# Moving the split weights by 64 bytes within SBUF

## The chip, the core and the metric

The kernel runs on one core of a Trainium2 chip. The metric is the device time of one execution, in microseconds (us); 1 ns is a thousandth of it. The profile of one execution shows what each engine did: TensorE (PE; its weight loads are PEld), VectorE (DVE), ScalarE (ACT), GpSimd (POOL) and SyncE (SP, which only issues DMAs).

## What is computed

One layer of a hybrid decoder for 576 tokens (512 of a prompt and 8 samples of 8), model width 1024, all in float32:

```
u   = rms(x) * g_pre_mix
z, xbc, dt, q, k, v, ig, fg, og = split(u @ w_in)       # one input projection
y_ssd = Mamba2-SSD heads(xbc, dt) gated by z;  h_ml = mLSTM heads(q, k, v, ig, fg) gated by og
x   = x + rms(concat(y_ssd, h_ml) @ w_out) * g_post_mix  # output projection
mk, mv = rms(mem) * g_mem @ w_mem_k, ... @ w_mem_v       # memory keys and values of the prompt
x   = x + rms(attention(rms(x) @ w_xq, mk, mv) @ w_xo) * g_post_x
x   = x + rms((silu(u @ w_gate) * (u @ w_up)) @ w_down) * g_post_ffn
```

The samples also read and update recurrent states and cached keys and values. The outputs are the new x, the memory keys and values and all new states.

## The kernel before

Nearly all of the work is matrix products in which both operands are split: a float32 value is the sum of a high part, rounded to the type float32r, and a low part, the difference. A product of two split operands takes three matmuls per tile of 128 x 128 weights, which accumulate in PSUM: high weights with high activations, high weights with low activations, low weights with high activations. In `gemm` (lines 194 to 205) these are lines 201, 202 and 204; each one is a matmul with a weight load of its own:

```
(wh, wl), ah, al = tiles[k], xh(k, t0, n), xl(k, t0, n)
mm(ps, wh, ah, start=i == 0, stop=False)
mm(ps, wh, al, start=False, stop=False)
```

In `mm(out, a, b)` the operand `a` is the stationary one (loaded into the array, 128 columns of 4 bytes) and `b` the moving one (streamed through it, `n` columns). In most products the weights are stationary and the activations move. In the memory values (lines 794 to 796) and in the mLSTM values v (line 814) the weights are the moving operand.

The 576 tokens are taken in two parts, of 256 and 320 columns, or, in the attention's output projection and the gated MLP, of 288 and 288. The input projection, the two output projections' halves, the query projection and the memory keys run unit by unit: a unit is 8 weight tiles of 128 x 128 (a 512 KB load), and gives 24 matmuls for each part of the tokens. The gated MLP forms products by sums and differences of its operands in blocks (class `Seven`, with `mul` at lines 1848 to 1850); its gate and up products begin in the plain form of lines 201 to 204.

The weights come by DMA into a tile `raw` (line 174), ScalarE writes the high part `whi` (line 179) and VectorE, or for the input projection partly a DMA that accumulates, the low part `wlo` (line 186). `raw`, `whi` and `wlo` lie in the pool "weights", each tile 4096 bytes per partition, in 2, 3 and 3 buffers. Another pool holds three more `whi` and `wlo` in the later stages, and `wacc`, `w3`, `wdh` and `wdl` are split weights in other places again.

The pools are laid out in SBUF one behind the other, in the order in which they are opened: "const" (from 16512), "weights" (from 18336), and "big" (from 51104), which has the activations' slots. The pool "const" holds constants and the small tiles of the reciprocal square roots: in `newton` and `root_sums` the tiles `v`, `y` and `a` in two buffers each, of up to 20 bytes, 32 bytes apart.

The start of an operand modulo 256, in bytes per partition. A weight tile of 128 columns is 512 bytes on from the one before it, and a token tile's row of 576 or 640 columns is 2304 or 2560 bytes, so the start modulo 256 does not depend on k. The second half of 288 columns starts 1152 bytes on, so there the moving operand's start is 128 more, modulo 256.

| tile | role | start modulo 256, before | after |
|---|---|---|---|
| `whi`, `wlo` of the pool "weights" | split weights | 160 | 96 |
| `whi`, `wlo` of the later pool, `wacc`, `w3`, `wdh`, `wdl` | split weights | 160 | 160 |
| `wmh` / `wml` | a memory key's weights, split | 224 / 160 | same |
| `uh`, `ul` | input projection, activations | 160 | same |
| `mixs_h` / `mixs_l` | first output projection (SSD half) | 224 / 160 | same |
| `mixm_h`, `mixm_l` | second output projection (mLSTM half) | 160 | same |
| `u2h`, `u2l`, `memhl` | query projection, memory | 160 | same |
| `qh` / `ql` | attention's output projection | 224 / 160 | same |
| `u3h`, `u3l`, `b1`, `b5` | gate and up products | 160 | same |
| `hh` / `hl` | down products | 224 / 160 | same |

The order of the instructions on each engine comes from a scheduler that works from dependencies and a cost model, and from an order written out by hand for the last stages.

Of the kernel before, what the change touches and what calls it, by code (L numbers as in the profile page):

```python
# [11 lines left out]
F32 = mybir.dt.float32  # L12
# [7 lines left out]
P = 128  # L20
# [95 lines left out]
def build(nc, tc, ctx, I, O):  # L116
# [2 lines left out]

    cp = ctx.enter_context(tc.tile_pool(name="const", bufs=1))  # L120
    wp = ctx.enter_context(tc.tile_pool(name="weights", bufs=1))
    big = ctx.enter_context(tc.tile_pool(name="big", bufs=1))
    pg = ctx.enter_context(tc.tile_pool(name="pg", bufs=3, space=PSUM))
    pa = ctx.enter_context(tc.tile_pool(name="pa", bufs=3, space=PSUM))
# [29 lines left out]
    def C32(k):  # L154
        a, b = _c32[k]
        return c32[:, a:b] if b <= NLONG else c32e[:, a - NLONG:b - NLONG]
# [64 lines left out]
    def rstd_cols(ssq, chunks, name, d=1024.0, alloc=None):  # L221

        nch = len(chunks)
        ps = (alloc or BP)("ps_ss")
        for j in range(nch):
            for i, t_ in enumerate(ssq):
                ssq_mm.append(mm(ps[:, j:j + 1], t_[:, chunks[j][0]:chunks[j][0] + P], ones, start=i == 0,
                                 stop=i == len(ssq) - 1, skip_group_check=True))
        return newton(ps[:, :nch], [P, nch], name, d)

    def newton(src, shape, name, d):
        v = cp.tile(shape, F32, name=name + "_v", tag="nt_v", bufs=2)
        y = cp.tile(shape, F32, name=name + "_y", tag="nt_y", bufs=2)
        a = cp.tile(shape, F32, name=name + "_a", tag="nt_a", bufs=2)
        r = cp.tile(shape, F32, name=name + "_r")
        w = shape[1]
        V.tensor_scalar(v, src, 1.0 / d, EPS, op0=ALU.mult, op1=ALU.add)
        pows.append(G.tensor_tensor(y, v, C32("nhalf")[:shape[0], :w], op=ALU.pow))
        V.tensor_tensor(a, y, y, op=ALU.mult)
        V.scalar_tensor_tensor(a, a, -0.5, v, op0=ALU.mult, op1=ALU.mult)  # L240
        rops.append(V.scalar_tensor_tensor(r, a, 1.5, y, op0=ALU.add, op1=ALU.mult))
        return r
# [339 lines left out]
    y = xs  # L582
# [126 lines left out]
    for g in range(2):  # L709
# [13 lines left out]
        for h in range(8):  # L723
            k, j = h % 2, (8 * g + h) // 2
# [163 lines left out]
    for h in range(4):  # L888
        q, k = qk[:, h, :], qk[:, 4 + h, :]
# [689 lines left out]
    def root_sums(name, ssq, i, alloc):  # L1579
        ps = alloc("ps_ss")  # L1580
        for c, (t0, _) in enumerate(ECHUNKS[i]):
            mm(ps[:, c:c + 1], ssq[:, t0:t0 + P], ones, start=True, stop=True, skip_group_check=True)
        v, y, a = [cp.tile([P, 3], F32, name=name + k, tag="nt" + k, bufs=2) for k in ("_v", "_y", "_a")]
        V.tensor_scalar(v, ps[:, :3], 1.0 / 1024.0, EPS, op0=ALU.mult, op1=ALU.add)
        G.tensor_tensor(y, v, C32("nhalf")[:, :3], op=ALU.pow)
        R[name] = v, y, a
# [19 lines left out]
    def norm(name, ssq, i, out, alloc, p, d):  # L1606

        at_(p, root_sums, name, ssq, i, alloc)
        at_(p + 0.4, root_step, name)
        at_(d, root_rows, name, i, alloc)  # L1610
        at_(d + 0.2, root_copy, name, i, out)
# [744 lines left out]
```

## Time and profile before

| | |
|---|---|
| three executions | 1095.28, 1095.61 and 1095.99 us; median 1095.61 |
| span of the profiled execution | 1095.0 us, from its first instruction to its last; no other time of that execution is listed |
| busy | PE 1084.1 us, PEld 1027.5, DVE 754.0, ACT 611.7, POOL 225.8 |
| matmuls | 8124, each with a weight load |
| DMA | 182.29 MB, mean 166 GB/s |

A row of instructions in the profile gives line, engine, operation, the tile written `<-` the tiles read (moving operand first), the shape and the count, then busy time in us and the mean duration of one in ns, then the idle time before them and what ended it. A row of the timeline gives the start in us from the span's start, the duration in us, and the instruction. The duration of a matmul covers its way through the array, so it overlaps with the next one's; the distance from one start to the next, the pitch, is what it takes of the time.

### The profile page before, as it was taken

Reading aid. Unit: us, or ns where it says so; the run is one execution under the profiler, and the core shown is the slowest. Engines: PE = TensorE matmul, PEld = TensorE weight load, DVE = VectorE, ACT = ScalarE, POOL = GpSimd, SP = SyncE. Lnnn points to the kernel's source line nnn. Section 1 sums busy time; section 2 is a strip of 40 time slices with the busy share of each in tenths; the row PEclk is TensorE's granted clock in tenths of the full one; section 3 lists DMA queues with packets and bytes.
Section 4 is the critical chain, followed back from the end, with each engine's and each line's share of the span. In section 5 each row is a group of like instructions: output and inputs, shape, how many; then the busy total and the mean of one; then the engine's idle time right before and its main releaser. Section 6 shows DMA issues by size and latency. Waiting matters only on the chain.

```text
span 1095.0 us, 20715 instructions
## 1 busy us (share of the span) xinstructions
PE 1084.1 (99%) x8124; PEld 1027.5 (94%) x8124; DVE 754.0 (69%) x1507; ACT 611.7 (56%) x1098; POOL 225.8 (21%) x305
## 2 busy tenths in 40 slices
PE   9999999999999999999999999999999999999997
PEld 8999887778999999999988879999999999999997
DVE  6896785658877775558744546676566877787555
ACT  7767632455654555656545445645566566656653
POOL 1332643313213112000144301100011121111000
PEclk9999999999999999999999999999999999999999
DMA  6785635435655349653467775644386687588532
GB/s 204 170 154 127 170 111 174 163 84 177 189 149 146 106 132 312 205 189 102 150 215 271 264 248 163 217 161 109 104 195 142 150 196 173 116 188 186 128 130 88
DMA packets 58967, 182.29 MB, mean 166 GB/s; under 512 B 6605, under 2 KB 11853, under 8 KB 58357
## 3 DMA queue, kind: packets, MB, share of 16 engines
q1 hardware_dynamic: 42740, 138.06, 39.0%
q0 software_dynamic: 15552, 41.95, 19.8%
q8 instruction: 64, 1.05, 0.4%
q10 hardware_dynamic: 576, 0.95, 0.3%
q14 instruction: 35, 0.28, 0.1%
HBM read 160.28 MB, written 20.65 MB: 165 GB/s over the span
## 4 chain that ended last, share of the span: by engine, by line
PE 88%; DVE 5%; ACT 4%; DMA 2%; issue 1%; SPq 0%; POOL 0%; DVEq 0%; ACTq 0%
PE ps_v L814 5%; PE ps_in L202 4%; PE ps_in L201 4%; PE ps_in L204 4%; PE ps_o L202 3%; PE ps_o L204 3%; PE ps_o L201 3%; PE ps_g L1848 3%; PE ps_g L1849 3%; PE ps_g L1850 3%; PE ps_u L1848 3%; PE ps_u L1850 3%; PE ps_u L1849 3%; PE ps_dn L1848 2%; PE ps_dn L1849 2%; PE ps_dn L202 2%
## 5 line engine op out<-in xcount | busy, mean ns | idle before, releaser
L201 PE MATMUL ps_in<-uh,whi 128*128 128x320 f32 (+1 forms) x544 | 164.0, 302 | 0.4 <-DVE cb L450 0.4
L204 PE MATMUL ps_in<-uh,wlo 128*128 128x320 f32 (+1 forms) x544 | 163.2, 300 | 0.0
L202 PE MATMUL ps_in<-ul,whi 128*128 128x320 f32 (+1 forms) x544 | 162.7, 299 | 0.0
L179 ACT CAST whi<-raw 128x1024 fp32r<-128x1024 f32 (+1 forms) x104 | 105.2, 1013 | 96.2 <-PE ps_in L202 26.1
L186 DVE TENSOR_TENSOR wlo<-raw,whi 128x512 fp32r<-128x512 f32 (+1 forms) x96 | 96.6, 1009 | 66.5 <-ACT whi L179 65.8
L201 PEld LDWEIGHTS ps_in<-uh,whi 128*128 128x128 f32 x544 | 103.1, 190 | 3.4 <-issue 1.7
L204 PEld LDWEIGHTS ps_in<-uh,wlo 128*128 128x128 f32 x544 | 103.0, 190 | 1.2 <-issue 0.4
L202 PEld LDWEIGHTS ps_in<-ul,whi 128*128 128x128 f32 x544 | 103.1, 190 | 0.6
L184 POOL DMA_DIRECT2D wlo<-win x32 | 27.9, 871 | 80.1 <-ACT wlo L183 72.0
L1848 PE MATMUL ps_g<-b,whi 128*128 128x288 f32 x144 | 42.5, 295 | 0.0
L1849 PE MATMUL ps_g<-b,whi 128*128 128x288 f32 x144 | 42.4, 295 | 0.0
L1848 PE MATMUL ps_u<-b,whi 128*128 128x288 f32 x144 | 42.4, 295 | 0.0
L1849 PE MATMUL ps_u<-b,whi 128*128 128x288 f32 x144 | 42.4, 295 | 0.0
L1821 ACT CAST whi<-rawx 128x1024 fp32r<-128x1024 f32 (+1 forms) x26 | 25.7, 987 | 27.8 <-PE ps_dn L1849 13.8
L191 DVE TENSOR_TENSOR wlo<-sw,whi 128x1024 fp32r<-128x1024 f32 (+1 forms) x26 | 29.6, 1140 | 14.9 <-ACT whi L190 14.7
L201 PE MATMUL ps_xo<-qh,whi 128*128 128x288 f32 x128 | 38.5, 302 | 0.2 <-ACT whi L179 0.2
L202 PE MATMUL ps_o<-mixs_l,whi 128*128 128x320 f32 (+1 forms) x128 | 38.2, 299 | 0.0
L204 PE MATMUL ps_o<-mixm_h,wlo 128*128 128x256 f32 (+1 forms) x128 | 38.2, 298 | 0.0
L202 PE MATMUL ps_o<-mixm_l,whi 128*128 128x256 f32 (+1 forms) x128 | 37.9, 296 | 0.0
L201 PE MATMUL ps_xq<-u2h,whi 128*128 128x320 f32 (+1 forms) x128 | 37.9, 300 | 0.0
L201 PE MATMUL ps_o<-mixm_h,whi 128*128 128x256 f32 (+1 forms) x128 | 37.9, 296 | 0.0
L204 PE MATMUL ps_xq<-u2h,wlo 128*128 128x320 f32 (+1 forms) x128 | 37.9, 296 | 0.0
(765 smaller groups left out, 3838.9 us busy)
## 6 DMA issues: line engine op xcount, KB each, us to landing
raw<-win SPq DMA_DIRECT2D x35, 512.0 KB, 3.9
raw<-wout SPq DMA_DIRECT2D x17, 512.0 KB, 3.6
raw<-wxq SPq DMA_DIRECT2D x13, 512.0 KB, 3.6
raw<-wgate SPq DMA_DIRECT2D x13, 512.0 KB, 3.5
raw<-wup SPq DMA_DIRECT2D x13, 512.0 KB, 5.3
wlo<-win POOLq DMA_DIRECT2D x24, 256.0 KB, 5.1
kva<-kc SPq DMA_DIRECT2D x12, 512.0 KB, 5.7
kva<-vc SPq DMA_DIRECT2D x12, 512.0 KB, 6.0
```

Source lines behind the costliest of these rows:

```text
L179: casts.append(A.copy(hi[:, :n], raw[:, :n]))
L184: G.dma_start(lo[:, a:b], src[:, a:b], accum_op=ALU.add)
L186: e.tensor_tensor(lo[:, a:b], raw[:, a:b], hi[:, a:b].bitcast(F32), op=ALU.subtract)
L191: (eng or V).tensor_tensor(lo, src, hi.bitcast(F32), op=ALU.subtract)
L201: mm(ps, wh, ah, start=i == 0, stop=False)
L202: mm(ps, wh, al, start=False, stop=False)
L204: m = mm(ps, tiles[order[c]][1], xh(order[c], t0, n), start=False, stop=c == len(tiles) - 1)
L814: mm(ps, a, b, skip_group_check=True, **kw)
L1821: A.copy(s.h3[:, s.all], s.r2[:, s.all])
L1848: mm(ps, wh, b[0][k], start=start and k == 0, stop=False, skip_group_check=True)
L1849: mm(ps, wh, b[1][k], start=False, stop=False, skip_group_check=True)
L1850: m = mm(ps, wl, b[0][k], start=False, stop=k == nk - 1, skip_group_check=True)
```

## The change

A pool "newton" is opened behind "weights", and the tiles `v` of `newton` and of `root_sums`, in two buffers of 32 bytes, move there from "const". "const" becomes 64 bytes shorter, so that the few small tiles behind `v` in it and the whole pool "weights" lie 64 bytes lower: `whi`, `wlo` and `raw` start at 96 modulo 256 in place of 160. The new pool fills the 64 bytes behind "weights", and every pool after it stays where it was. The instructions and their order on each engine are the same.

```diff
     cp = ctx.enter_context(tc.tile_pool(name="const", bufs=1))
     wp = ctx.enter_context(tc.tile_pool(name="weights", bufs=1))
+    nv = ctx.enter_context(tc.tile_pool(name="newton", bufs=1))
     big = ctx.enter_context(tc.tile_pool(name="big", bufs=1))
...
     def newton(src, shape, name, d):
-        v = cp.tile(shape, F32, name=name + "_v", tag="nt_v", bufs=2)
+        v = nv.tile(shape, F32, name=name + "_v", tag="nt_v", bufs=2)
         y = cp.tile(shape, F32, name=name + "_y", tag="nt_y", bufs=2)
...
             mm(ps[:, c:c + 1], ssq[:, t0:t0 + P], ones, start=True, stop=True, skip_group_check=True)
-        v, y, a = [cp.tile([P, 3], F32, name=name + k, tag="nt" + k, bufs=2) for k in ("_v", "_y", "_a")]
+        v, y, a = [(nv if k == "_v" else cp).tile([P, 3], F32, name=name + k, tag="nt" + k, bufs=2) for k in ("_v", "_y", "_a")]
         V.tensor_scalar(v, ps[:, :3], 1.0 / 1024.0, EPS, op0=ALU.mult, op1=ALU.add)
```

## The prediction

> **What bounds the kernel now.** I read the page's busy shares, the chain that ended last, the waits of TensorE, the sums by window, and then the timeline of TensorE product by product. From the page:
>
> ```profile
> span 1095.0 us, 20715 instructions
> ...
> PE 1084.1 (99%) x8124; PEld 1027.5 (94%) x8124; DVE 754.0 (69%) x1507; ACT 611.7 (56%) x1098; POOL 225.8 (21%) x305
> ...
> PEclk9999999999999999999999999999999999999999
> ...
> PE 88%; DVE 5%; ACT 4%; DMA 2%; issue 1%; SPq 0%; POOL 0%; DVEq 0%; ACTq 0%
> ```
>
> TensorE is busy for 99% of the span, at full clock in every slice, and makes 88% of the chain. Its waits, of which the first and the last of six rows stand here, are next to nothing:
>
> ```profile
> PE ps_warm L302 <- DVE wz L299: 1.1, 1, 1.1
> ...
> PE ps_xo L201 <- ACT whi L179: 0.2, 1, 0.2
> ```
>
> So the time is the sum of the distances from the start of one matmul to the start of the next. Only a change of that pitch can move the end by much, and this change touches nothing else: all five engines issue the same instructions in the same order; some operands lie 64 bytes lower. The profiled span of 1095.0 is 0.6 under the median of 1095.61; I take differences from the profile and set them against the median.
>
> **What a pitch is made of.** "Distance" below is the start address of the moving operand less that of the stationary operand of the next matmul (which loads meanwhile), modulo 256. In the second product of the output projection, mixm_h, mixm_l and the weights all start at 160 modulo 256: distance 0. In the first, mixs_h starts at 224, so two products of three are at distance 64 and the third, of mixs_l, at 0. Both run without a stall, each unit being 24 matmuls of 256 columns and then 24 of 320. From the timeline, the first row of each run of 24 and of what follows it:
>
> ```profile
> 411.36 0.28 PE L201 MATMUL ps_o<-mixs_h,whi 128*128 128x256 f32 x1
> ...
> 414.21 0.31 PE L201 MATMUL ps_o<-mixs_h,whi 128*128 128x320 f32 x1
> ...
> 417.73 0.28 PE L201 MATMUL ps_o<-mixs_h,whi 128*128 128x256 f32 x1
> ...
> 453.13 0.28 PE L201 MATMUL ps_o<-mixm_h,whi 128*128 128x256 f32 x1
> ...
> 456.01 0.31 PE L201 MATMUL ps_o<-mixm_h,whi 128*128 128x320 f32 x1
> ...
> 459.53 0.28 PE L201 MATMUL ps_o<-mixm_h,whi 128*128 128x256 f32 x1
> ```
>
> At distance 0, 24 matmuls of 256 columns take 456.01 - 453.13 = 2.88 us, 120.0 ns each; with two in three at 64 they take 2.85 us, 118.75 each. That is 1.25 ns a matmul over all, or 1.9 ns for each one that is at 64. At 320 columns both take 3.52 us, 146.7 each: no gain. The mean durations of the groups, between 403 and 453 us, show the same and a little more:
>
> ```profile
> L202 PE MATMUL ps_o<-mixs_l,whi 128*128 128x320 f32 x53 | 16.6, 312 | 0.0
> L201 PE MATMUL ps_o<-mixs_h,whi 128*128 128x320 f32 x53 | 16.4, 309 | 0.0
> L204 PE MATMUL ps_o<-mixs_h,wlo 128*128 128x320 f32 x53 | 16.3, 308 | 0.0
> L202 PE MATMUL ps_o<-mixs_l,whi 128*128 128x256 f32 x48 | 13.7, 285 | 0.0
> L204 PE MATMUL ps_o<-mixs_h,wlo 128*128 128x256 f32 x48 | 13.4, 280 | 0.0
> L201 PE MATMUL ps_o<-mixs_h,whi 128*128 128x256 f32 x48 | 13.4, 279 | 0.0
> L201 PE MATMUL ps_o<-mixm_h,whi 128*128 128x320 f32 x16 | 4.9, 309 | 0.0
> ...
> L201 PE MATMUL ps_o<-mixm_h,whi 128*128 128x256 f32 x8 | 2.3, 283 | 0.0
> ```
>
> A duration is longer than a pitch, since matmuls overlap, but its differences can be compared. At 256 columns the products of mixs_h are 3.5 under the 283 of distance 0 and that of mixs_l is 2 over it; at 320 they are 0.5 under and 3 over. A second case at 256 columns is the memory keys: memhl at 160, weights wmh at 224 (distance 192), wml at 160; 48 matmuls:
>
> ```profile
> 496.32 0.28 PE L201 MATMUL ps_mk<-memhl,wmh 128*128 128x256 f32 x1
> ...
> 501.98 0.28 PE L794 MATMUL ps_v<-wmh,memhl 128*128 128x256 f32 x1
> ```
>
> 5.66 us over 48 is 117.9 ns, 2.1 under 120.0. At 288 columns distance 0 is not the dear one. The first half of the gate and up products has distance 0, the second, from 724.28 on, 128, since the half's offset is 1152 bytes; the output projection of the attention has 64, 0, 64:
>
> ```profile
> 717.43 0.29 PE L204 MATMUL ps_g<-u3h,wlo 128*128 128x288 f32 x1
> ...
> 724.28 0.29 PE L201 MATMUL ps_g<-u3h,whi 128*128 128x288 f32 x1
> ...
> 749.88 0.29 PE L1848 MATMUL ps_g<-u3h,whi 128*128 128x288 f32 x1
> ...
> 655.62 0.30 PE L201 MATMUL ps_xo<-qh,whi 128*128 128x288 f32 x1
> ...
> 658.40 0.29 PE L201 MATMUL ps_xo<-qh,whi 128*128 128x288 f32 x1
> ```
>
> 52 matmuls at distance 0 take 6.85 us, 131.7 each; 192 at distance 128 take 25.60, 133.3 each; 21 of the mixture take 2.78, 132.4 each.
>
> **The sum.** Counted in the two programs, pair by pair of single-pass products:
>
> - 256 columns, 0 to 64: 1469 pairs. I take 1.9 ns off each, from the unit above: -2.8 us. The ends are no gain and 2.1 (the keys): 0 to -3.1.
> - 256 columns, 0 to 192 (the memory values, where the split weights are the moving operand): 138 pairs, also 1.9: -0.3; ends 0 and -0.3.
> - 320 columns, 0 to 64: 1321 pairs. The equal 3.52 us says 0. A gain as large as the keys' 2.1 would be -2.8; the other end is the dearest run of 320 columns at 64, 0, 64, that of the last down product, below: +3.0.
> - 288 columns: 850 pairs go from 0 to 64. The run at 64, 0, 64 is 0.7 above distance 0: +0.6; the ends are 0 and the 1.6 between 131.7 and 133.3: +1.4. 596 pairs go from 128 to 192, 253 from 192 to 0, 209 from 64 to 128. By the same step of 1.6 the first two can bring -1.0 and -0.4 and the third can cost +0.3; I take -0.2 for all three.
> - 256 and 320 columns, 64 to 128, in the mixed products: 213 and 214 pairs. No row has 128 at these widths; by the step of 1.6 either way, within 0.7 us; I take 0.
> - 512 columns, 0 to 192 (the values): 203 pairs, none of them to be compared in a stream; at most 2.1 ns either way, 0.4 us; I take 0.
>
> The remaining 1340 or so pairs keep their distance: tiles of other pools, among them another pool of split weights. The sum is -2.8 - 0.3 + 0 + 0.6 - 0.2 = -2.7 us: **1092.9**.
>
> What else the move touches costs nothing in time that I can see. The casts and subtractions that fill the split weights, and their loads, keep their sizes and order; the moved tiles are 8 to 20 bytes per partition. A faster TensorE could be held up by its supply; a unit of 48 matmuls, 6.4 us, stands against these:
>
> ```profile
> L179 ACT CAST whi<-raw 128x1024 fp32r<-128x1024 f32 (+1 forms) x104 | 105.2, 1013 | 96.2 <-PE ps_in L202 26.1
> L186 DVE TENSOR_TENSOR wlo<-raw,whi 128x512 fp32r<-128x512 f32 (+1 forms) x96 | 96.6, 1009 | 66.5 <-ACT whi L179 65.8
> ...
> raw<-win SPq DMA_DIRECT2D x35, 512.0 KB, 3.9
> ```
>
> About 1 us of cast, 1 us of subtraction and 3.9 us to landing are covered by the unit in work, and 0.03 or 0.1 us less of it leaves them covered. Without cover a unit could be no faster than its load, 3.9 us, far from here.
>
> **The rivals.** *A: the gain is larger.* Once both activations lie at one distance, the stream no longer jumps between two, and the 2 and 3 ns over at mixs_l (285 and 312) may belong to the jump. Then each 256-column pair gains the 3.5 of mixs_h and each 320-column pair 0.5: 1607 x 3.5 + 1321 x 0.5 = 5.6 + 0.7, less the 0.4 lost at 288: -5.9, so 1089.7. Against it: the equal 3.52 us at 320, and the keys, where the moving operand does not jump and gains only 2.1.
>
> *B: addresses do not count.* The two operands are read without regard to each other, and the differences between stages come from something else in them. Then nothing moves: 1095.6. The memory keys speak against it, at 117.9 with an ordinary stream, as does the step from 131.7 to 133.3 within one set of products at 724.28; for it speaks the equality at 320. The Trainium skill has this as a rule: "SBUF — State Buffer", section "Who interferes with whom", gives TensorE two independent read ports, one for the moving operand and one for weight loads, and says that TensorE never waits for anyone. The trace agrees at 320 columns (3.52 us in both) and not at 256 (2.85 against 2.88).
>
> *C: slower.* Distance 64 is dear where most bytes stream, at 288 and 320 columns. The last down product has the distances 64, 0, 64 against the tile wdh; 21 matmuls of 320 columns:
>
> ```profile
> 1061.81 0.31 PE L201 MATMUL ps_dn<-hh,wdh 128*128 128x320 f32 x1
> ...
> 1064.94 0.28 PE L201 MATMUL ps_dn<-hh,wdh 128*128 128x256 f32 x1
> ```
>
> 3.13 us is 149.0 each, 2.3 above 146.7. If the 320-column pairs become like these, +3.0 us, the 288-column ones like distance 128, 850 x 1.6 = +1.4, and a stream wholly at 64 keeps the 120.0 at 256, the sum is +4.4: 1100.0. It is decided at 320 columns: with the gain of 3.1 at 256 kept and 1.4 lost at 288, it ends slower than now from 1.3 ns a pair. For it: no large product in the trace starts its weights at 96, where they will lie. Against it: the run of 24 at 64, 0, 64 in the first output projection shows no such cost, at 3.52 us.
>
> **How the numbers follow.** My forecast has 0.36, A 0.18, B 0.18, C 0.28. Each term's ends added up reach -8.0 and about +5; the range that leaves out two in ten goes from 1086 to 1100, which takes in A and C. A measurement can tell about 0.2% from no change, 2.2 us. Faster by more than that are most of the forecast (0.30), A and a little of B (0.02): 0.50. Within it are the rest of the forecast (0.06) and of B (0.16): 0.22. Slower is C: 0.28.
>
> **What would show it.** Right: the 24 matmuls of 256 columns in the second output projection take 2.84 us or less and those of 320 columns 3.52, and the first half of the gate and up products goes up from 131.7 towards 132.4. A shows as under 2.82 and under 3.50; C as over 3.55; B as 2.88 and 3.52 with 1095.6 in all. Waits of TensorE that sum to over 10 us, or a chain with less of TensorE in it, would make the whole argument wrong, since then the pitch would not set the time.

## The result and the profile after

| | before | after |
|---|---|---|
| median of ten executions each, same chip | 1096.10 us | 1093.55 us |
| ratio, 95% interval | | 0.9978 [0.9969, 0.9987] |
| span of the profiled execution | 1095.0 us | 1090.7 us |

The changed kernel is faster by 0.22%, which is close to the least that a measurement of this kernel can tell from no change; the interval excludes no change. The prediction said 1092.9. The spans show more of a gain than the medians do. The profiled execution of after took 1092.51 us, the least of its ten; and where a run lists both, the time is 1.7 to 1.9 us over the span, so the span of 1095.0 belongs to some 1096.8 us, over the median of before. A second profile of after (below) has 1092.2.

From the page of the kernel after:

```profile
span 1090.7 us, 20715 instructions
...
PE 1081.4 (99%) x8124; PEld 1024.5 (94%) x8124; DVE 753.3 (69%) x1507; ACT 611.6 (56%) x1098; POOL 227.0 (21%) x305
...
PE 90%; DVE 4%; DMA 2%; issue 2%; ACT 2%; POOL 0%; SPq 0%; DVEq 0%; ACTq 0%; POOLq 0%
```

TensorE is busy for 99% as before and has 90% of the chain (88% before). Its waits, all of them:

```profile
PE ps_warm L303 <- DVE wz L300: 1.1, 1, 1.1
PE ps_ct L554 <- ACT r L533: 0.3, 1, 0.3
PE ps_in L205 <- DMA wlo<-win: 0.2, 1, 0.2
PE ps_xo L202 <- ACT whi L180: 0.2, 1, 0.2
```

They sum to 1.8 us. Before, they summed to 3.3; these are the four rows of before that the prediction does not show:

```profile
PE ps_ss L227 <- DVE ssqx L268: 0.8, 1, 0.8
PE ps_in L338 <- ACT whi L190: 0.5, 1, 0.5
PE ps_in L201 <- DVE cb L450: 0.4, 1, 0.4
PE ps_ct L553 <- ACT r L532: 0.3, 1, 0.3
```

In the second profile of after they sum to 4.3 us. They vary from one execution to the next by about as much as the change is worth, but all are far under the 10 us that the prediction set as the sign against it: the supply of weights kept up, and the pitch still sets the time. The timeline of TensorE in after, with the first row of each run of equal products and of what follows it (lines 202, 203 and 205 are 201, 202 and 204 of before):

```profile
409.53 0.28 PE L202 MATMUL ps_o<-mixs_h,whi 128*128 128x256 f32 x1
...
412.33 0.31 PE L202 MATMUL ps_o<-mixs_h,whi 128*128 128x320 f32 x1
...
450.95 0.28 PE L202 MATMUL ps_o<-mixm_h,whi 128*128 128x256 f32 x1
...
453.77 0.31 PE L202 MATMUL ps_o<-mixm_h,whi 128*128 128x320 f32 x1
...
457.30 0.28 PE L202 MATMUL ps_o<-mixm_h,whi 128*128 128x256 f32 x1
...
493.79 0.28 PE L202 MATMUL ps_mk<-memhl,wmh 128*128 128x256 f32 x1
...
499.45 0.28 PE L795 MATMUL ps_v<-wmh,memhl 128*128 128x256 f32 x1
...
713.88 0.29 PE L202 MATMUL ps_u<-u3h,whi 128*128 128x288 f32 x1
...
720.60 0.29 PE L202 MATMUL ps_g<-u3h,whi 128*128 128x288 f32 x1
...
746.19 0.30 PE L1849 MATMUL ps_g<-u3h,whi 128*128 128x288 f32 x1
...
1057.55 0.31 PE L202 MATMUL ps_dn<-hh,wdh 128*128 128x320 f32 x1
...
1060.67 0.28 PE L202 MATMUL ps_dn<-hh,wdh 128*128 128x256 f32 x1
```

In the second output projection (mixm) the 24 matmuls of 256 columns take 453.77 - 450.95 = 2.82 us (2.88 before), and the 24 of 320 columns 3.53 (3.52). In the first (mixs) the 256 columns take 2.80 (2.85). The memory keys, whose addresses did not change, take 5.66 us, as before. The first half of the gate and up products takes 6.72 us over 51 matmuls, 131.8 ns each (131.7), the second 25.59 over 192, 133.3 each (133.3). The last down product, unchanged too, takes 3.12 us over 21 (3.13). The gain sits at 256 columns, as forecast.

Where time was won and where it was lost is seen in the groups by form. In the input projection at 256 columns a matmul of the high parts went from 288 to 286 ns; in the mLSTM values, where the weights stream 512 columns, it went from 404 to 408. Two rows of before, then two of after (line, engine, operation, count, then busy us and mean ns of one):

```profile
L201 PE MATMUL ps_in<-uh,whi 128*128 128x256 f32 x272 | 78.2, 288 | 0.0
L814 PE MATMUL ps_v<-whi,uh 128*128 128x512 f32 x80 | 32.2, 404 | 0.0
```

```profile
L202 PE MATMUL ps_in<-uh,whi 128*128 128x256 f32 x272 | 77.7, 286 | 0.1
L815 PE MATMUL ps_v<-whi,uh 128*128 128x512 f32 x80 | 32.5, 408 | 0.0
```

Worked out over all starts in the two traces, matmul by matmul, with the pairs that stall in either trace left out:

| columns, distance before to after | pairs | pitch before, ns | after, ns | us in all | forecast, us |
|---|---|---|---|---|---|
| 256, 0 to 64 | 1431 | 120.35 | 118.16 | -3.13 | -2.8 |
| 256, 0 to 192 | 135 | 121.24 | 118.09 | -0.43 | -0.3 |
| 320, 0 to 64 | 1300 | 147.80 | 147.48 | -0.41 | 0 |
| 288, 0 to 64 | 849 | 132.36 | 132.11 | -0.21 | +0.6 |
| 288, 128 to 192, 192 to 0, 64 to 128 | 1050 | | | -0.41 | -0.2 |
| 256 and 320, 64 to 128 | 426 | | | +0.10 | 0 |
| 512, 0 to 192 | 199 | 234.51 | 237.72 | +0.64 | 0 |
| 288, 0 unchanged | 495 | | | +0.24 | none made |

The rows add up to -3.6 us, more than the 2.55 us between the medians; the next run shows where the rest went.

### The profile page after: what moved, and what is told of

The parts are those of the page before. It is cut to its first block, busy times and chain, and to the rows that moved or that the text cites. A ratio compares the mean times of both kernels' runs of the same rounds, so it can differ in the third digit from the quotient of the medians.

```text
span 1090.7 us, 20715 instructions
## 1 busy us (share of the span) xinstructions
PE 1081.4 (99%) x8124; PEld 1024.5 (94%) x8124; DVE 753.3 (69%) x1507; ACT 611.6 (56%) x1098; POOL 227.0 (21%) x305
## 4 chain that ended last, share of the span: by engine, by line
PE 90%; DVE 4%; DMA 2%; issue 2%; ACT 2%; POOL 0%; SPq 0%; DVEq 0%; ACTq 0%; POOLq 0%
PE ps_in L203 5%; PE ps_in L202 5%; PE ps_in L205 5%; PE ps_v L815 3%; PE ps_o L205 3%; PE ps_o L203 3%; PE ps_o L202 3%; PE ps_u L1850 3%; PE ps_g L1850 3%; PE ps_g L1849 3%; PE ps_u L1851 3%; PE ps_g L1851 3%; PE ps_u L1849 3%; PE ps_dn L1849 2%; PE ps_dn L1851 2%; PE ps_dn L1850 2%
## 5 line engine op out<-in xcount | busy, mean ns | idle before, releaser
L180 ACT CAST whi<-raw 128x1024 fp32r<-128x1024 f32 (+1 forms) x104 | 105.2, 1013 | 95.6 <-PE ps_in L203 25.9
L202 PE MATMUL ps_o<-mixs_h,whi 128*128 128x320 f32 (+1 forms) x128 | 37.7, 295 | 0.0
L1801 ACT CAST whi<-raw 128x1024 fp32r<-128x1024 f32 (+1 forms) x26 | 25.6, 984 | 21.6 <-PE ps_g L1850 9.6
L203 PE MATMUL ps_xo<-ql,whi 128*128 128x288 f32 x128 | 37.6, 295 | 0.0
```

What stands on the lines that cost most here:

```text
L180: casts.append(A.copy(hi[:, :n], raw[:, :n]))
L1801: s.c1 = A.copy(s.h1[:, s.all], s.r1[:, s.all])
```

## The experiments

All twelve kernels compute the whole layer and issue the instructions of before; they differ in where tiles lie. Ratios are against the kernel before on the same chip. "O" is the distance of a moving operand from its own stationary operand, as "D" is the prediction's, from that of the next matmul; "W" is the theory that the place of the weights counts by itself, and "S" that a whole stream falls into one of a few periods. The table gives the mean pitches of streams without a stall, in ns, worked out from the starts in each trace: the input projection (u) and the second output projection (mixm), the first half of the gate and up products (u3), and the mLSTM values (512 columns, weights moving).

| kernel | start of whi / wlo | ratio [95%] | u, 256 | mixm, 256 | u, 320 | u3, 288 | 512 |
|---|---|---|---|---|---|---|---|
| before | 160 / 160 | 1 | 119.5 | 119.8 | 147.5 | 132.3 | 234.5 |
| after | 96 / 96 | 0.9978 [0.9969, 0.9987] | 117.5 | 117.8 | 147.5 | 132.5 | 237.7 |
| e3_both_lower (activations at 96 too) | 96 / 96 | 0.9983 [0.9974, 0.9992] | 119.5 | 119.8 | 147.6 | 131.9 | 234.9 |
| e8_distance_32 | 128 / 128 | 0.9999 [0.9991, 1.0008] | 117.2 | 116.9 | 147.5 | 133.5 | 237.4 |
| e12_distance_96 | 64 / 64 | 1.0012 [1.0003, 1.0021] | 119.4 | 119.8 | 147.8 | 132.7 | 238.0 |
| e4_distance_128 | 32 / 32 | 1.0004 [0.9995, 1.0013] | 118.7 | 118.6 | 147.6 | 132.9 | 236.7 |
| e7_distance_192 | 224 / 224 | 0.9965 [0.9952, 0.9977] | 116.0 | 116.1 | 147.4 | 133.3 | 234.7 |
| e11_distance_224 | 192 / 192 | 0.9997 [0.9988, 1.0006] | 118.3 | 118.1 | 147.5 | 133.0 | 237.4 |
| e2_high_only | 96 / 160 | 0.9964 [0.9952, 0.9977] | 117.9 | 117.8 | 146.3 | 132.7 | 237.2 |
| e9_low_only | 160 / 96 | 0.9975 [0.9966, 0.9985] | 118.0 | 117.9 | 146.9 | 132.3 | 235.0 |
| e10_high_only_192 | 224 / 160 | 0.9999 [0.9990, 1.0008] | 118.1 | 117.8 | 147.6 | 133.4 | 236.4 |
| e5_high224_low96 | 224 / 96 | 0.9951 [0.9939, 0.9964] | 115.1 | 113.6 | 146.3 | 133.2 | 235.4 |
| e6_low224_high96 | 96 / 224 | 0.9968 [0.9956, 0.9980] | 117.2 | 115.6 | 146.8 | 132.4 | 235.9 |

### The changed kernel once more: e1_after_again

No edit.

> The changed kernel again, beside the three kernels that follow. In the stall-free runs of the second output projection, 24 matmuls of 256 columns should take 2.82 us (117.6 ns each) and 24 of 320 columns 3.52 us, against 2.88 and 3.52 before; in all a ratio of 0.998 to the kernel before, about 2.4 us less.

It took 1094.02 us, 0.9982 [0.9973, 0.9991], with a span of 1092.2. Class by class its trace repeats the table above almost to the digit: -3.11 us at 256 columns, 0 to 64, and +0.64 at 512. The streams repeat; what lies between them and in the stalls does not (all that is no single-pass stream differs from before by -2.16 us in the first profile, by +0.28 in this one; the stalled pairs by +1.6 and +0.7; the waits sum to 1.8 and 4.3 us). So the extra 1.5 us of the first profile's gain are that execution's own. The profiled execution here, 1094.04 us, is at the median of its eleven: in it the streams give some 3.7 us, of which about 1 us is lost again at the joints and stalls. Each is one execution, so the 1 us is rough.

### Is it the place or the distance? e3_both_lower

The new pool is opened behind "big", so that the activations' slots move down with the weights: both start at 96.

```diff
     wp = ctx.enter_context(tc.tile_pool(name="weights", bufs=1))
-    nv = ctx.enter_context(tc.tile_pool(name="newton", bufs=1))
     big = ctx.enter_context(tc.tile_pool(name="big", bufs=1))
+    nv = ctx.enter_context(tc.tile_pool(name="newton", bufs=1))
```

> The split weights and the activations of the pool behind them both lie 64 bytes lower: the weights start at 96 modulo 256 as in the changed kernel, but uh, ul, mixm and u2 start at 96 too, and their distance is 0 as before. Theory D: the run of 24 matmuls of 256 columns in the second output projection is back at 2.88 us, and the time at about that of before, within 1.5 us (memhl, in another pool, stays at distance 64 and keeps some 0.4 us). Rival W (the weights' own place counts, 160 is dear and 96 is not): the run stays at 2.82 us and the time 2.4 us lower, ratio 0.998.

```profile
446.45 0.28 PE L202 MATMUL ps_o<-mixm_h,whi 128*128 128x256 f32 x1
...
449.32 0.31 PE L202 MATMUL ps_o<-mixm_h,whi 128*128 128x320 f32 x1
...
452.85 0.28 PE L202 MATMUL ps_o<-mixm_h,whi 128*128 128x256 f32 x1
```

In the timeline of e3 the 24 matmuls of 256 columns are back at 2.87 us and those of 320 take 3.53: with the weights at 96 as in after, but the activations there too, the pitch is that of before. For this stream the place of the weights by itself does nothing; the distance does. It is the stream that decides, not the time in all: the whole kernel was still 1.9 us faster than before, which is outside the 1.5 us that D allowed, and by its ratio, 0.9983, e3 can't be told from after (0.9982). The memory products explain more than half of it: memhl stays at 160 and the weights go to 96, so the distance becomes 64 for the keys (119.2 to 116.6 ns) and 192 for the values (119.2 to 115.6), about 1.1 us.

### Other distances for both weights: e4, e7, e8, e11, e12

Each moves more or fewer of the small tiles behind "weights". e4 moves `v` and `y`, e7 `v`, `y` and `a`, e8 only the tile `r` named "rx", e12 `v` and that `r`, e11 all four. The main lines of e7's edit against before, then of e8's, which opens the same pool; the line of `root_sums` changes like that of `newton` and is not shown, and the others combine these lines:

```diff
+    nv = ctx.enter_context(tc.tile_pool(name="newton", bufs=1))
...
-        v = cp.tile(shape, F32, name=name + "_v", tag="nt_v", bufs=2)
-        y = cp.tile(shape, F32, name=name + "_y", tag="nt_y", bufs=2)
-        a = cp.tile(shape, F32, name=name + "_a", tag="nt_a", bufs=2)
+        v = nv.tile(shape, F32, name=name + "_v", tag="nt_v", bufs=2)
+        y = nv.tile(shape, F32, name=name + "_y", tag="nt_y", bufs=2)
+        a = nv.tile(shape, F32, name=name + "_a", tag="nt_a", bufs=2)
```

```diff
-        r = cp.tile(shape, F32, name=name + "_r")
+        r = (nv if name == "rx" else cp).tile(shape, F32, name=name + "_r")
```

> The pool of the weights lies 128 bytes lower than before (start 32): distance 128 where it was 0, 192 where it was 64, 0 where it was 128. Theory D in the form 'any distance but 0 will do': the run of 256 columns takes 2.82 us again and the time falls by 2 to 3 us. Rival D2 ('0 and 128 are alike, 64 and 192 are alike', as if the period were 128): the run is back at 2.88 us, and the time within 1 us of that of before. At 288 columns the first half of the gate and up products should show the 133.3 ns that distance 128 has in the second half before, +1.6 ns for 850 matmuls or +1.4 us, and where the second half's distance falls to 0 it should show 131.7, -1.6 ns for some 600 or -1.0 us.

> The pool of the weights lies 192 bytes lower than before: distance 192 where it was 0. Theory D by the memory keys of the kernel before (distance 192 in two of three, 117.9): 117.8 at 256 columns in the input and output projections, 146.7 at 320, and a ratio near 0.998. If the side counts (the moving operand ahead of the weights by 64 against behind by 64), 256 columns differ from the 117.5 to 117.8 of distance 64 by over 0.5 ns either way.

> The pool of the weights lies 32 bytes lower than before: distance 32. Pitches at 256 columns so far: 119.8 at distance 0, 117.8 at 64, 118.5 at 128. If the pitch goes smoothly with the distance: 118.8, and a ratio of 0.999. If what counts is blocks of 64 bytes, so that 32 bytes leave half of the conflict: as distance 0, 119.8, ratio 1.000. If an offset of half a block is worse than either: over 120, and slower than before.

> The pool of the weights lies 224 bytes lower: distance 224, which is 32 bytes the other way. Distance 32 gave 116.9 at 256 columns in the second output projection but nothing in all, since 288 and 512 columns lost as much. If the two sides are alike: the same, ratio 1.000. If the side counts as it did for 64 against 192 (0.998 against 0.9965): under 0.999.

> The pool of the weights lies 96 bytes lower: distance 96. If whole steps of 64 bytes are what TensorE likes and the odd multiples of 32 cost at 288 and 512 columns as 32 did: 117 to 118 at 256 columns, 133.4 in the first half of the gate and up products, and a ratio of 0.999 to 1.001. If the pitch at 256 columns goes smoothly between distance 64 (117.8) and 128 (118.5), 118.1, and a ratio of 0.999.

At distance 128 the kernel keeps half of the gain at 256 columns (-1.7 us, 0 to 128) and loses 1.0 us at 288 (849 pairs, 132.3 to 133.5) and 0.4 at 512: no change in all. This is the step of 1.6 ns between the two halves of the gate products, at 1.2 here. Distance 192 is the best for both weights together: -5.1 us at 256 columns, nothing lost at 512. The three odd multiples of 32 that were tried gain nothing in all. At 32 the 256 columns gain more than at 64 (-3.6 us, 116.9 ns in mixm), but 288 columns cost +0.9, those at 288 that kept their distance +0.45, and 512 columns +0.6. At 96 even the 256 columns stay at 119.8, and the kernel is 0.12% slower than before. So a distance off zero isn't good by itself, and each width has its own good ones. Few of the expectations held. In e4 neither form did, since 118.6 ns lies between the 2.82 us and the 2.88 us that they named. In e7 the side counts: 116.1 ns against the 117.8 of distance 64. No expectation had the 116.9 of e8 or the 119.8 of e12. In e11 the two sides are alike in the time in all, but not at 256 columns (118.1 against 116.9). Distance 160 for both weights was not tried, nor were the small tiles moved without the weights. That distances count modulo 256 was assumed; 0 and 128 do differ (119.8 and 118.6), and inside one run of after, where the distance also grows by multiples of 256, the pitch is 117.8 ns at each of them.

The timeline of e7 in the second output projection shows something else:

```profile
443.47 0.28 PE L202 MATMUL ps_o<-mixm_h,whi 128*128 128x256 f32 x1
...
446.20 0.30 PE L202 MATMUL ps_o<-mixm_h,whi 128*128 128x320 f32 x1
...
449.72 0.28 PE L202 MATMUL ps_o<-mixm_h,whi 128*128 128x256 f32 x1
...
452.54 0.31 PE L202 MATMUL ps_o<-mixm_h,whi 128*128 128x320 f32 x1
```

One run of 24 takes 2.73 us, the next one 2.82: 113.8 and 117.5 ns, with the same tiles at the same distances. The means between them in the table (116.1 here, 115.6 in e6) are mixtures of two such levels. The weights take three buffers in turn, so the fourth unit of 256 columns has all its operands and its place in PSUM at the same addresses as the first, the run of 2.73 us. It takes 2.83:

```profile
462.41 0.28 PE L202 MATMUL ps_o<-mixm_h,whi 128*128 128x256 f32 x1
...
465.24 0.31 PE L202 MATMUL ps_o<-mixm_h,whi 128*128 128x320 f32 x1
```

### One weight moved: e2, e9, e10

The pool "weights" is split in two, one for `whi` and one for `wlo`, with small tiles between. e2 has the high parts at 96 and the low parts at 160; e9 opens the low pool first, and has the reverse; e10 has all of `v`, `y` and `a` between, so that the high parts lie at 224. `raw` lies in the pool that stays at 160. The core of e2:

```diff
-    wp = ctx.enter_context(tc.tile_pool(name="weights", bufs=1))
+    wp = ctx.enter_context(tc.tile_pool(name="high", bufs=1))
+    nv = ctx.enter_context(tc.tile_pool(name="newton", bufs=1))
+    lp = ctx.enter_context(tc.tile_pool(name="low", bufs=1))
...
-        hi, lo = [(pool or wp).tile([P, 1024], F32R, name=k, tag=k, bufs=NWX if pool else 3) for k in ("whi", "wlo")]
+        hi, lo = [(pool or (wp if k == "whi" else lp)).tile([P, 1024], F32R, name=k, tag=k, bufs=NWX if pool else 3) for k in ("whi", "wlo")]
```

> Only the high weights of the pool lie 64 bytes lower (start 96 modulo 256); the low weights and raw stay at 160. Theory D (the distance between a moving operand and the stationary operand that loads meanwhile, that of the next matmul): the products of lines 'high x high' and 'low x high' are followed by a high weight and are at distance 64, the product 'high x low' is followed by the low weight and stays at 0. So the first and the third of each triple gain about 2 ns at 256 columns and the second nothing: a run of 24 takes 2.84 to 2.85 us, and the time falls by about two thirds of the 3.6 us that 256 columns gave, 2 us, ratio 0.9982 to 0.9985. Theory O (the distance to the matmul's own stationary operand): the first and the second gain, the third does not. The total is the same by both; which of the three pitches falls tells them apart.

> Only the low weights of the pool lie 64 bytes lower (96 modulo 256); the high weights and raw stay at 160. Of the three products of a triple, only the third (low weights, high activations) has its own weights at another place than the activations, and only the second (high weights, low activations) is followed by them. With only the high weights lower, the first two pitches fell and the third did not. Theory O (the own stationary operand): now the third falls alone, by some 2 to 3 ns at 256 columns, and the time by a third of that kernel's 3.9 us, ratio near 0.9988. Theory D (the next one's): the second falls alone, with the same total. Theory S (a stream falls into one of a few fixed periods per triple, whose single pitches mean little): any of the three may fall, and the period of a triple at 256 columns is near the 353 of the kernel with only the high weights lower; at 320 columns it is under the 440 of equal places, as it was there (436).

> Only the high weights move, to 224 modulo 256; the low weights and raw stay at 160. It differs from the best kernel so far (high 224, low 96, ratio 0.995) only in the low weights' place. Theory S: what makes the lowest pitch of 113.3 ns at 256 columns is weights on both sides of the activations, so here it is not reached, 117 to 118 and a ratio near 0.9965, as with only the high weights at 96. If the high weights at 224 do it alone, 113 to 115 at 256 columns and a ratio near 0.995.

The timeline of e2, and its groups by form for the same product (lines 203, 204 and 206 are the three matmuls):

```profile
450.43 0.28 PE L203 MATMUL ps_o<-mixm_h,whi 128*128 128x256 f32 x1
...
453.25 0.31 PE L203 MATMUL ps_o<-mixm_h,whi 128*128 128x320 f32 x1
...
456.74 0.28 PE L203 MATMUL ps_o<-mixm_h,whi 128*128 128x256 f32 x1
```

```profile
L206 PE MATMUL ps_o<-mixm_h,wlo 128*128 128x256 f32 x64 | 18.2, 285 | 0.0
L204 PE MATMUL ps_o<-mixm_l,whi 128*128 128x256 f32 x64 | 17.9, 280 | 0.0
L203 PE MATMUL ps_o<-mixm_h,whi 128*128 128x256 f32 x64 | 17.8, 279 | 0.0
```

With one weight of two moved, the 24 matmuls of 256 columns take 2.82 us, just as with both. Inside the triple the gain is at the two lines that stream against the moved weight (279 and 280 ns, the third 285). From the starts, the pitches of lines 203, 204 and 206 are 116.0, 117.2 and 120.3; in e9 118.6, 119.2 and 115.6. By D, line 204 of e2 should have stayed, since the next weight is the unmoved one, and 206 should have fallen; the reverse is seen. So D as a rule for the single matmul falls, and here O tells which line gets shorter. But O doesn't tell the amount: in this product a triple takes 353 to 354 ns whether one (e9), two (e2) or three (after) of its matmuls are off zero. What is set is the period of the stream, and the lines share it. So each fell by more than its expectation: 0.9964 in e2 for 0.9982 to 0.9985, and 0.9975 in e9 for 0.9988.

At 320 columns the mixture gains what a common distance didn't: 24 matmuls take 456.74 - 453.25 = 3.49 us, and the input projection goes from 147.5 to 146.3. This is the main part of what makes e2 better than after. e10 has the gain at 256 columns in mixm and u, and no more: 320 columns stay at 147.6, the first output projection loses 1.2 ns at 256, the gate products 1.0 at 288, and the values 1.9 at 512. It ends where before did: the 117 to 118 ns that were expected came, the ratio of 0.9965 didn't.

The first output projection of e10 also shows that O is no rule either. There mixs_h and the high weights start at 224, mixs_l and the low weights at 160: by D all three products are at distance 0, by O only the first is (0, 192, 64).

```profile
404.86 0.28 PE L203 MATMUL ps_o<-mixs_h,whi 128*128 128x256 f32 x1
...
407.74 0.31 PE L203 MATMUL ps_o<-mixs_h,whi 128*128 128x320 f32 x1
```

The 24 matmuls take 2.88 us, as at distance 0 in mixm before, so here the period goes with D. And the line that O has at 64 is the longest: the pitches are 117.6, 118.5 and 123.2 ns. D alone doesn't fix the period either: with the distances 64, 0, 64 by D, mixm in e2 takes 2.82 us and mixs in before 2.85. So neither distance alone is the rule; that the starts of all the operands in a triple count together is a guess, which no run tests.

### The two weights on two sides: e5, e6

e5 puts the high parts at 224 and the low parts at 96, 64 to either side of the activations: `v` and `y` lie between the two pools, `a` behind them. e6 is its mirror.

```diff
+    wp = ctx.enter_context(tc.tile_pool(name="high", bufs=1))
+    nb = ctx.enter_context(tc.tile_pool(name="newton2", bufs=1))
+    lp = ctx.enter_context(tc.tile_pool(name="low", bufs=1))
+    nv = ctx.enter_context(tc.tile_pool(name="newton", bufs=1))
...
+        v = nb.tile(shape, F32, name=name + "_v", tag="nt_v", bufs=2)
+        y = nb.tile(shape, F32, name=name + "_y", tag="nt_y", bufs=2)
+        a = nv.tile(shape, F32, name=name + "_a", tag="nt_a", bufs=2)
```

> The high weights of the pool start at 224 modulo 256 and the low ones at 96, so that they lie 64 on either side of the activations at 160. In the run with both lower, the memory keys had just this arrangement (memhl 160, wmh 224, wml 96) and took 113.3 ns a matmul of 256 columns, where distance 64 alone gave 117.8 and distance 0 119.8. Theory S (the weights on two sides let a stream run at the lowest of a few fixed pitches): 113.3 at 256 columns in the input and output projections, 6.5 ns off some 1600 matmuls or 10 us, and perhaps 140 in place of 146.7 at 320, as much again: 1078 to 1086 us, ratio 0.984 to 0.991. Theory D (each matmul by its own distance, 64 and 192 being worth 2 ns at 256 columns): like the changed kernel, 117.5 and a ratio of 0.998.

> The mirror image: the low weights start at 224 and the high ones at 96 modulo 256. Theory S, if only the two sides count: the same as with high at 224 and low at 96. If the order of the three products counts (high x high, high x low, low x high, so that two of three weight tiles are the high ones), the pitch differs from that kernel's, and one of the two is near the 118.0 of the kernel with only the high weights lower. Theory D: 117.5 at 256 columns and a ratio of 0.998, as in the changed kernel.

The timeline of e5:

```profile
450.98 0.28 PE L204 MATMUL ps_o<-mixm_h,whi 128*128 128x256 f32 x1
...
453.70 0.30 PE L204 MATMUL ps_o<-mixm_h,whi 128*128 128x320 f32 x1
...
457.19 0.28 PE L204 MATMUL ps_o<-mixm_h,whi 128*128 128x256 f32 x1
```

The 24 matmuls of 256 columns take 2.72 us, 113.3 ns each, and those of 320 columns 3.49. e5 took 1090.24 us, 0.9951 [0.9939, 0.9964]: it beats both kernels and is the best found. The expectation of 113.3 at 256 columns held; that of 140 at 320 didn't (146.3), so the total missed its range, which ended at 1086. Class by class it gains 6.7 us at 256 columns and 1.6 at 320, and gives back 2.7 us in pairs that stall in one trace or the other. e6 is between: its runs in the second output projection take 2.73 us or 2.85, two levels as in e7, so the two sides alone don't make the lowest pitch last.

### The same tiles at two pitches

Two stretches of the memory keys in the profile of after; both rows of a pair lie in one run without a stall, and between the two runs other matmuls came:

```profile
608.74 0.28 PE L205 MATMUL ps_mk<-memhl,wlo 128*128 128x256 f32 x1
...
611.09 0.28 PE L203 MATMUL ps_mk<-memhl,whi 128*128 128x256 f32 x1
...
613.38 0.28 PE L202 MATMUL ps_mk<-memhl,whi 128*128 128x256 f32 x1
...
614.63 0.28 PE L205 MATMUL ps_mk<-memhl,wlo 128*128 128x256 f32 x1
```

20 matmuls in 2.35 us are 117.5 ns each; 11 in 1.25 us are 113.6. Tiles and addresses modulo 256 are the same. So, as the two units of e7 showed, the addresses alone don't fix the pitch: within one arrangement a stream can run at either of two. Over all arrangements the full runs of 24 matmuls of 256 columns in the second output projection took 2.72 to 2.75 us (113 to 115 ns; e5, some in e6 and e7), 2.80 to 2.85 (117 to 119), or 2.87 to 2.88 (120; before, e3, e12). The lowest are set apart; the others lie close together and are no sharp levels. What picks the level wasn't found.

## Why the prediction was right, point by point

- **The pitch sets the time**: right. The waits of TensorE summed to 3.3 us before and to 1.8 and 4.3 us in the two profiles of after, TensorE stayed at 99% busy, and the change of the time is that of the streams, less about 1 us at joints and stalls.
- **The total**: the medians differ by 2.55 us, the forecast was 2.7. That it came so close is in part luck: the streams gave 3.6 to 3.7 us, and about 1 us of it, which the sum had no term for, didn't reach the end. Inside the streams the misses at 288 columns (0.8 us better than forecast) and at 512 (0.64 worse) nearly cancel.
- **256 columns, 0 to 64**: right, -3.1 us for -2.8, or 2.2 ns a pair for the 1.9 taken from the mixed unit. It came out a little over the bound taken from the memory keys, 2.1. The 24 matmuls took 2.82 us, within the "2.84 or less" that was to show it.
- **256 columns, 0 to 192**: right, -0.4 for -0.3.
- **320 columns**: right in the main; 3.52 or 3.53 us in mixm, and -0.4 us in all for the 0 taken.
- **288 columns**: the sign of the first term was wrong, -0.2 for +0.6, and the first half of the gate products did not rise from 131.7 towards 132.4 (131.8). The step failed that took one run of 21 matmuls at 64, 0, 64 for the price of a stream wholly at 64. The three other classes gave -0.4 for -0.2; the 495 pairs whose distance didn't change, put at nothing, cost 0.2. e4 shows that the cost that it feared exists at distance 128: 1.2 ns a pair.
- **512 columns**: mis-sized. It was set at 0 within 0.4 us, with the step of 256 columns as the bound; it cost 3.2 ns each, 0.64 us in all. No row stood behind the bound but one of another width, with the operands' roles the other way round.
- **The mechanism**: that the two operands' addresses count together is right (e3). D, the distance to the next matmul's stationary operand, is wrong as the price of one matmul (e2 and e9); it goes with the period in the first output projection of e10, but does not fix it. In a common shift of both weights D and O give nearly the same counts of pairs (1469 and 1477 for 256 columns, 0 to 64), so the sum couldn't tell them apart.
- **The ends**: the ends of the terms add up to about -8.7 and +5.8 us, not to -8.0 and about +5. The range did not rest on them.
- **Rival A** was not seen in after (2.82 and 3.53 us for the two runs of 24, where it named less than 2.82 and 3.50), and its reason, that a stream gains by one distance throughout, isn't borne out: the lowest pitch was had in e5, with two distances in each triple, and at 320 columns the mixture in e2 gained what the common distance didn't.
- **Rival B** falls. e3 restores the distance and with it the pitch of before, with the weights where after has them; e5 is 0.5% faster by addresses alone. The Trainium skill's rule ("SBUF — State Buffer", "Who interferes with whom"), two independent read ports and a TensorE that never waits, doesn't agree with these runs: 119.8, 117.8 and 113.6 ns for the same 256-column products. Whether it is at the ports that the two operands meet, no run here shows.
- **Rival C** didn't come at distance 64; in e12, at 96, a slower kernel did, 1.0012 [1.0003, 1.0021], with only -0.35 us at 256 columns, 0 to 96, and +0.7 us at 512, a width that C had not named.

## What to carry to other kernels

When TensorE is busy for 99% and waits for nothing, look at the pitch of each stream from start to start, by width and by the start addresses of both operands modulo 256; moving tiles by 32 to 224 bytes changed the time by +0.1% to -0.5% here, with the same instructions. Try several arrangements, the parts of a split weight on two sides of the activations among them, and count each width apart: what 256 columns gain, 288 or 512 can lose. Take a profile twice before a gain of 2 us is credited, and compare streams rather than spans.

## What was not expected of the hardware

The pitch is set for a whole stream, not matmul by matmul: in the second output projection a triple of 256 columns takes the same 353 to 354 ns whether one weight of two lies 64 lower or both. Within one execution the same kind of product at the same addresses modulo 256 ran at 117.5 and at 113.6 ns, two microseconds apart, and in e7 two units with all addresses equal took 2.73 and 2.83 us. At 320 columns a common distance of 64 did next to nothing (147.8 to 147.5 over all pairs), while different starts for the high and the low weights gave 146.3 in the input projection in e2 and e5, 146.8 and 146.9 in e6 and e9, and nothing in e10 (147.6). None of the runs tells why.
